# One-hop convolution shifts, scan pooling, paired output tiles and a GpSimd power for the norm scales, in an eight-core encoder step

## The chip, the cores and the metric

The kernel runs as one program on all eight cores of a Trainium2 chip; cores 0 to 3 are one die, 4 to 7 the other. Each core takes its own part of the tokens. The metric is the device time of the slowest core in microseconds (us). Engines are named as in the profile: PE (TensorE matmuls), PEld (weight loads of TensorE), DVE (VectorE), ACT (ScalarE), POOL (GpSimd), SP (SyncE). L405 means line 405 of the kernel in question, so the same statement can have another number in another kernel.

The runs here fell into two states. In a slow run the cores of one die, or of both, show a lower granted TensorE clock than in the others, and the run is longer. All verdicts here compare fast runs with fast runs of the same chip and the same rounds.

## The reference, cut to what matters

Four layers, each with another token mixer, on x of D = 1024 channels; inner width E = 2048:

```python
def rms_norm(x, g):
    y = xf * lax.rsqrt(jnp.mean(xf * xf, axis=-1, keepdims=True) + EPS)
    return y * g
...
for i in range(4):
    h = rms_norm(x, g_norm[i]) * (1.0 + scale) + shift
    # 0: gMLP   1: short conv   2: GLU -> depthwise conv of 31 taps -> LayerNorm -> silu
    # 3: trailing means over 2, 4, 8, 16 positions, one per channel group, minus the token
    x = x + gate * einsum(y * silu(z), w_out[i])
return rms_norm(x, g_final), ...
```

Every `rsqrt` is of one number per token.

## The kernel before

Activations are transposed: channels on the 128 partitions, tokens along the free dimension. A core works through its tokens in two groups, of 1074 columns (three matmuls of 358) and 1056 (three of 352); the groups take turns, layer by layer. PE writes to two PSUM slots of three banks each, so at most two output tiles are open. Weights come through a ring of eight 512 KB slots that POOL's queue loads.

The norm of the next layer is woven as "hooks" into the eight output tiles `d` of the *other* group's output projection, so that PE has work while the norm is made:

```python
hooks = {0: [sq(0..7)],                     # ACT: squares
         1: [stats(0..7), rstd],            # PE: column sums into bank 6; then the scale
         3: [bc, apply(0)],                 # PE: spread the scale over 128 partitions
         4..6: two applications each, 7: one}
...
def rstd():                                 # q96 is [96, W]: 3 thirds of the tokens, 32 equal rows each
    dve.tensor_scalar_add(q96, PSB[0:96, 6, 0:W], EPS)
    dve.reciprocal(q96, q96)
    act.activation(q96, q96, Sqrt)
def bc():                                   # matmul with sel = 1/32 over the 32 equal rows
    for q in range(3): matmul(PSB[:, slot, 0:W], lhsT=sel[32*q:32*q+32, :], rhs=q96[32*q:32*q+32, :])
    act.activation(rb, PSB[:, slot], Copy)
```

The column sums come as 32 identical rows per third of the tokens. The LayerNorm of layer 2 (`finalize`) has the same reciprocal and root. The output projection finishes tile after tile; only its first tile takes its 16 products one by one as they become ready:

```python
for d in range(8):
    sl = next_slot()
    if d == 0: for e in eorder: tile_mm(sl, w[e], ys[e])     # waits per e
    else:      tile_mm(sl, all 16)
    dve: x[d] += gate * PSUM                                  # the eviction
    for fn in hooks[d]: fn()
```

The convolution of 31 taps runs on PE with four shifted copies of the data. Their making went through DRAM:

```python
sp.dma(g_dram[c % 4], G)                                      # hop 1: write 280 KB
for sft in range(4):                                          # hop 2: read back, shifted
    sp.dma(R[32*sft:32*sft+32, :, 0:RW], AP(g_dram, offset + sft, [[GW, 32], [32*GW, 4], [1, RW]]))
```

Pooling adds shifted copies, doubling the window each time (one add for 2, four for 16):

```python
while step < win:
    dve.tensor_tensor(d_[lo:wd], cur[lo:wd], cur[lo-step:wd-step], add);  step *= 2
```

## Time and profile before

| | before |
|---|---|
| runs | 2359.1, 2494.44 (slow), 2360.89 us |
| span of the profiled cores | 2344.8 to 2353.8 us, core 1 slowest |
| PE / DVE / ACT / POOL busy | 94 / 47 / 27 / 8% |
| sum of PE gaps of 0.6 us and more, core 1 (added up from PE's timeline) | 128.6 us, 45 of them in the first 370 us |

First the page of the kernel before: busy us with the share of the span, PE's busy tenths in 40 slices, and the shares of the chain that ended last.

```profile
PE 2202.8 (94%) x16875; PEld 1360.6 (58%) x16875; DVE 1097.1 (47%) x1603; ACT 634.4 (27%) x726; POOL 193.1 (8%) x336
...
PE   4999999989999999999999999899988989998995
...
PE 80%; DVE 8%; DMA 7%; ACT 2%; issue 2%; SPq 0%; POOL 0%; DVEq 0%; ACTq 0%; POOLq 0%
```

PE is busy almost everywhere, and the chain is PE's for four fifths. A change that removes no matmul can only close PE's gaps. What PE waits for is listed by releaser: us in total, how often, the longest.

```profile
PE ps L452 <- DVE ysT L951: 12.9, 8, 2.6
PE ps L886 <- DMA tmp<-gscr: 12.7, 6, 4.0
PE ps L452 <- ACT tmp L914: 10.6, 4, 4.8
PE ps L452 <- ACT tmp L1036: 9.3, 8, 2.0
...
PE ps L452 <- DVE xb_sb L512: 5.6, 4, 1.4
PE ps L452 <- DVE xa_sb L512: 4.9, 5, 1.3
```

These are small sums: products of layer 2 that come too slowly for its output projection (L951), the read-back of the shifted copies (gscr), the eviction held up at layer 2's statistics (L914), the eviction held up by the pooling adds (L1036), and the ordinary waits of an output projection for an eviction (L512). The timeline shows the third of them. Columns: start, duration, engine, line, operation, and in brackets the idle time before it and what ended it.

```profile
1420.94 2.39 DVE L924 RECIPROCAL tmp<-tmp 96x358 f32<-96x358 f32 x1
...
1423.40 1.28 ACT L925 ACT_TABLE_LOAD   x1 [4.21 <-DVE tmp L924]
1424.69 0.50 ACT L925 ACTIVATE tmp<-tmp 96x358 f32<-96x358 f32 x1
1425.22 1.28 ACT L914 ACT_TABLE_LOAD   x1
...
1427.72 6.43 PE L452 MATMUL ps<-hT,ring 128*128 128x358 bf16 x24 [4.80 <-ACT tmp L914]
```

The scale of 96x358 values costs 2.39 us of reciprocal, 0.50 us of root, and two loads of ACT's function table of 1.28 us. ACT could not evict the tile that PE had finished, so PE stood 4.80 us. The windows view: us, PE busy and count, the same for PEld, DVE, ACT, POOL, then the granted clock, DMA's share and GB/s.

```profile
1427.72:1431.72 4.00, 4.00 (x14) 2.06 (x15) 1.28 (x1) 0.81 (x1) 0.00 (x0) 0.50 0.00 0
1435.72:1439.72 4.00, 4.00 (x28) 2.54 (x26) 3.24 (x3) 2.16 (x3) 0.00 (x0) 1.00 0.00 0
```

What the trace has on a power (POOL's only arithmetic in this kernel, in groups: operation and shapes, count, busy us, mean ns of one, idle before):

```profile
L681 POOL TENSOR_TENSOR stat<-stat 128x1 f32<-128x1 f32 x17 | 23.1, 1359 | 136.7 <-DVE stat L680 136.7
```

It is a power of one column. Pooling, in PE's timeline of the 16-wide channels:

```profile
1914.87 7.52 PE L452 MATMUL ps<-hT,ring 128*128 128x358 bf16 x48 [1.40 <-ACT tmp L1036]
```

48 matmuls take 7.52 us, and then PE waits, since four adds of about 1.29 us and the rest of DVE's work take longer than that (the next tile starts 8.92 us after this one). Last, the shift copies in the list of DMA issues: count, KB each, median us from issue to landing.

```profile
tmp<-gscr SPq DMA_DIRECT2D x64, 278.5 KB, 5.6
...
gscr<-tmp SPq DMA_DIRECT2D x32, 280.0 KB, 7.3
```

### The profile page before, as it was taken

How to read it: one execution, taken by the hardware profiler on the slowest of the kernel's cores; microseconds unless marked ns; L12 is line 12 of the kernel's file. 1: busy time of each engine (PE TensorE's matmuls, PEld its weight loads, DVE VectorE, ACT ScalarE, POOL GpSimd, SP SyncE). 2: the span in 40 equal slices, each digit the busy share in tenths (PEclk: the TensorE clock that was granted, in tenths of full speed). 3: DMA queues.
4: the chain of work that ended last, by engine and by line, in shares of the span. 5: the costliest groups of instructions: out<-in, count | busy, mean ns of one | idle time of the engine just before them, and what ended most of it. 6: DMA issues, size and time to landing. Idle time of an engine off the chain costs nothing.

```text
span 2353.8 us, 41088 instructions; the slowest of 8 cores (2344.8 to 2353.8 us)
## 1 busy us (share of the span) xinstructions
PE 2202.8 (94%) x16875; PEld 1360.6 (58%) x16875; DVE 1097.1 (47%) x1603; ACT 634.4 (27%) x726; POOL 193.1 (8%) x336
## 2 busy tenths in 40 slices
PE   4999999989999999999999999899988989998995
PEld 2645655446666666666666665566655656665663
DVE  3354230642555545555552216552328476456645
ACT  2354312633011120111202235312345122212221
POOL 1012101121001000010000000000000000000000
PEclk9999999999999999999999999999999999999998
DMA  9907738077346443464447773558765334433424
GB/s 205 207 7 110 124 64 133 1 132 120 55 71 108 72 82 54 75 110 77 82 84 176 174 163 52 88 117 179 170 129 90 63 63 72 66 63 61 72 50 145
DMA packets 75639, 233.36 MB, mean 99 GB/s; under 512 B 9728, under 2 KB 10368, under 8 KB 75296
## 3 DMA queue, kind: packets, MB, share of 16 engines
q0 software_dynamic: 44928, 163.60, 41.6%
q1 hardware_dynamic: 30528, 67.15, 11.4%
q8 instruction: 136, 2.23, 0.4%
q14 instruction: 47, 0.39, 0.1%
HBM read 375.57 MB, written 18.73 MB: 168 GB/s over the span
## 4 chain that ended last, share of the span: by engine, by line
PE 80%; DVE 8%; DMA 7%; ACT 2%; issue 2%; SPq 0%; POOL 0%; DVEq 0%; ACTq 0%; POOLq 0%
PE ps L452 69%; PE ps L654 5%; PE ps L886 4%; DVE tmp L1056 3%; DMA gscr<-tmp 2%; DMA ring<-w_in_a 2%; DMA tmp<-gscr 2%; DMA ring<-w_ada 1%; DVE tmp L1063 1%; PE ps L723 1%; ACT tmp L1036 1%; PE ps L719 1%; DVE xb_sb L512 1%; DMA xa_sb<-xa 0%; PE ps L398 0%
## 5 line engine op out<-in xcount | busy, mean ns | idle before, releaser
L452 PE MATMUL ps<-hT,ring 128*128 128x358 bf16 (+1 forms) x8448 | 1311.2, 316 | 38.5 <-ACT tmp L914 10.6
L452 PEld LDWEIGHTS ps<-hT,ring 128*128 128x128 bf16 x8448 | 826.6, 98 | 515.1 <-issue 59.8
L452 PE MATMUL ps<-ysT,ring 128*128 128x352 bf16 (+1 forms) x3072 | 476.2, 315 | 22.3 <-DVE ysT L951 12.9
L452 PEld LDWEIGHTS ps<-ysT,ring 128*128 128x128 bf16 x3072 | 298.6, 98 | 199.6 <-issue 32.5
L886 PE MATMUL ps<-tmp 128*32 128x358 bf16 (+1 forms) x3072 | 129.0, 324 | 12.8 <-DMA tmp<-gscr 12.7
L847 DVE TENSOR_TENSOR tmp<-tmp,ps 128x1074 bf16<-128x1074 f32 (+3 forms) x64 | 45.4, 709 | 186.8 <-PE ps L452 183.5
L654 PE MATMUL ps<-ring,hT 128*128 128x512 bf16 (+1 forms) x576 | 127.1, 379 | 3.9 <-DMA ring<-w_in_a 2.6
L886 PEld LDWEIGHTS ps<-tmp 128*32 128x32 bf16 x3072 | 84.3, 98 | 55.6 <-issue 22.6
L512 DVE SCALAR_TENSOR_TENSOR xb_sb<-ps,modT,xb_sb 128x704 f32<-128x704 f32 (+2 forms) x96 | 56.1, 584 | 127.0 <-PE ps L452 120.3
L789 DVE TENSOR_TENSOR tmp<-tmp,ps 128x1074 f32<-128x1074 f32 (+3 forms) x64 | 45.4, 710 | 140.3 <-PE ps L452 136.6
L1056 DVE TENSOR_TENSOR tmp<-tmp 128x1088 f32<-128x1088 f32 (+5 forms) x80 | 102.8, 1285 | 5.1 <-DVE tmp L1056 0.2
L1036 ACT ACTIVATE tmp<-ps 128x1074 f32<-128x1074 f32 (+3 forms) x64 | 39.4, 616 | 242.1 <-PE ps L452 164.2
L891 ACT ACTIVATE ysT<-ps,cst_sb 128x1074 bf16<-128x1074 f32 (+3 forms) x64 | 45.2, 706 | 206.8 <-PE ps L886 203.8
L779 ACT ACTIVATE tmp<-ps 128x1074 f32<-128x1074 f32 (+1 forms) x32 | 33.9, 1059 | 247.9 <-PE ps L452 173.9
L512 DVE SCALAR_TENSOR_TENSOR xa_sb<-ps,modT,xa_sb 128x1074 f32<-128x1074 f32 x32 | 42.7, 1335 | 123.0 <-PE ps L452 123.0
L654 PEld LDWEIGHTS ps<-ring,hT 128*128 128x128 bf16 (+1 forms) x576 | 55.5, 98 | 68.9 <-issue 4.9
L806 DVE SCALAR_TENSOR_TENSOR tmp<-tmp,cst_sb 128x1074 f32<-128x1074 f32 (+1 forms) x64 | 85.1, 1329 | 6.7
L810 ACT ACTIVATE ysT<-ps 128x1074 bf16<-128x1074 f32 (+1 forms) x32 | 33.9, 1059 | 184.2 <-PE ps L452 184.1
L452 PE MATMUL ps<-tmp,ring 128*128 128x358 bf16 (+1 forms) x384 | 63.2, 323 | 12.6 <-DVE ysT L1015 8.9
L741 DVE TENSOR_TENSOR ysT<-ysT,tmp 128x1074 bf16<-128x1074 bf16 (+1 forms) x32 | 22.8, 714 | 106.4 <-ACT tmp L740 106.4
L813 DVE TENSOR_TENSOR tmp<-tmp,ps 128x1074 f32<-128x1074 f32 (+3 forms) x64 | 45.4, 709 | 55.7 <-PE ps L452 52.0
L872 DVE TENSOR_TENSOR tmp<-dmask,cst_sb 128x1024 bf16<-128x1024 bf16 x32 | 39.2, 1225 | 59.1 <-PE ps L886 56.9
(151 smaller groups left out, 1562.9 us busy)
## 6 DMA issues: line engine op xcount, KB each, us to landing
ring<-w_in_b POOLq DMA_DIRECT2D x64, 512.0 KB, 5.4
ring<-w_ada POOLq DMA_DIRECT2D x48, 512.0 KB, 9.7
ring<-w_in_a POOLq DMA_DIRECT2D x48, 512.0 KB, 13.2
ring<-w_in_c POOLq DMA_DIRECT2D x48, 512.0 KB, 7.2
tmp<-gscr SPq DMA_DIRECT2D x64, 278.5 KB, 5.6
tmp<-gscr SPq DMA_DIRECT2D x64, 275.5 KB, 5.9
ring<-w_in_d POOLq DMA_DIRECT2D x32, 512.0 KB, 5.2
gscr<-tmp SPq DMA_DIRECT2D x32, 280.0 KB, 7.3
```

The lines of the kernel that those rows point to most:

```text
L452: ins = h.matmul(PSB[:, 3 * sl + n, 0:W], lhsT=lw, rhs=rh[:, n * W:(n + 1) * W], start=(first and k == 0), stop=(last and k == len(pairs) ...
L512: s.op("dve", lambda h, ps=ps, xv=xv, smp=smp, d=d: h.scalar_tensor_tensor(out=xv, in0=ps, scalar=gate[:, 16 + d, smp:smp + 1], in1=xv, op ...
L654: ins = h.matmul(PSB[0:n, nq, :], lhsT=hT[:, kh * 4 + kk, hc:hc + n], rhs=vw[nq * 2 + kh][:, kk, :], start=(kh == 0 and kk == 0), stop=(kh ...
L789: s.op("dve", lambda h, ps=ps, cc=cc, n=n, nb=nb, smp=smp, p=p, CG=CG: h.tensor_tensor(out=shp(p[:, H + cc + smp * H:H + cc + smp * H + n] ...
L806: s.op("dve", lambda h, p=p, a=a, c=c, wd=wd, k=k: h.scalar_tensor_tensor(out=a[:, 0:wd], in0=p[:, k:k + wd], scalar=prmT[:, c, k:k + 1], ...
L813: s.op("dve", lambda h, ps=ps, cc=cc, n=n, nb=nb, smp=smp, a=a, CG=CG: h.tensor_tensor(out=shp(tf(CG + cc, n), nb), in0=shp(a[:, cc + smp ...
L847: s.op("dve", lambda h, ps=ps, cc=cc, n=n, nb=nb, smp=smp: h.tensor_tensor(out=shp(G[:, H + cc + smp * H:H + cc + smp * H + n], nb), in0=s ...
L872: s.op("dve", lambda h: h.tensor_tensor(out=wd, in0=mk, in1=wrepT[:, c, :].unsqueeze(2).broadcast_to([128, 32, 32]), op=ALU.mult), reads=[ ...
L886: ins = h.matmul(PSB[32 * j:32 * j + 32, 3 * sl + n, 0:WC], lhsT=wd[:, b, j, :], rhs=R[:, j, 4 * b + n * WC:4 * b + (n + 1) * WC], start=( ...
L891: s.op("act", lambda h, ps=ps, cc=cc, n=n, nb=nb: h.activation(out=shp(ysT[:, c, cc:cc + n], nb), in_=ps, func=AF.Identity, bias=prmT[:, c ...
L1036: s.op("act", lambda h, ps=ps, cc=cc, n=n, nb=nb, smp=smp, pv=pv: h.activation(out=shp(pv[:, H + cc + smp * H:H + cc + smp * H + n], nb), ...
L1056: s.op("dve", lambda h, d_=d_, cur=cur, lo=lo, step=step: h.tensor_tensor(out=d_[:, lo:wd], in0=cur[:, lo:wd], in1=cur[:, lo - step:wd - s ...
```

## The change

The intent was to free PE of its gaps: shifts in one hop from SBUF to SBUF, pooling in one scan instead of up to four adds, two output tiles filled in turn so that PE has twice the work per product that arrives, and the scales as `x ** -0.5` on POOL, which has little to do, so that DVE loses a reciprocal and ACT a root with its table loads. The norm's hooks move back by one tile to fit the pairs. The diff, cut:

```diff
 def rstd():
     dve.tensor_scalar_add(q96, PSB[0:96, 6, 0:W], EPS)
-    s.op("dve", lambda h: h.reciprocal(out=q96, in_=q96), ...)
-    s.op("act", lambda h: h.activation(out=q96, in_=q96, func=AF.Sqrt), ...)
+    s.op("pool", lambda h: h.tensor_tensor(out=q96, in0=q96, in1=stat[0:96, 20:21].broadcast_to([96, W]), op=ALU.pow), ...)
 # ... the same in finalize() of layer 2; stat[:, 20] holds -0.5

 # output projection
+first = [next_slot(), next_slot()]
+for i, e in enumerate(eorder):
+    for d in range(2):
+        tile_mm(first[d], WT[g], [(ws[d][0][:, e, :], ysT[:, e, 0:NCOL[g]])], ..., i == 0, i == 15)
 for d in range(8):
-    ... one tile at a time, d == 0 by single e
+    ... d < 2: already done; else one tile at a time

 # norm hooks
-    1: stats + rstd,  3: bc, apply(0),  4..6: two applications each, 7: one
+    2: stats + rstd,  4: bc, apply(0),  5: apply 1, 2, 3,  6: 4, 5,  7: 6, 7

 # conv shifts
-s.dma("sp", ..., g_dram[c % 4], G, ...)
-for sft in range(4): s.dma("sp", ..., R[32*sft:32*sft+32, :, 0:RW], AP(g_dram, offset + sft, [[GW, 32], [32*GW, 4], [1, RW]]))
+for j in range(4):
+    g = G[32*j:32*j+32, 0:RW]
+    s.dma("sp", ..., R[:, j, 0:RW], AP(g.tensor, g.offset, [g.ap[0], [1, 4], [1, RW]]))
 # ... mask and tap layout permuted to match

 # pooling
-while step < win: dve.tensor_tensor(add); step *= 2
+if win == 2: dve.tensor_tensor(out=cur, in0=pv, in1=pad[PD-1:...], add)
+else:        dve.tensor_tensor_scan(out=cur, data0=pv, data1=pad[PD-win:...], op0=add, op1=subtract)
 # ... three input buffers instead of two; ACT copies the history
```

More of the change, by code (lines that the diff above doesn't have):

```diff
@@ L203, in build_program @@
         st_out[l] = (dout(nm + "_p", [128, 16 * HIST[l]]), dout(nm + "_s", [128, 16 * HIST[l]]))
-    g_dram = [nc.dram_tensor("gscr%d" % i, [128, GW], BF16, kind="Internal").ap() for i in range(4)]
     s = Sched(nc)
@@ L328, in build_program, with f_mask @@
     s.op("act", lambda h: h.activation(out=sc32[:, :, 0:2], in_=cT, func=AF.Silu), reads=["cst0", "sc32"], writes=["sc32"])
-    for q in range(4):
-        s.op("dve", lambda h, q=q: h.tensor_copy(out=dmask[32 * q:32 * q + 32, :], in_=ident[32 * q:32 * q + 32, 32 * q:32 * q + 32]),
-             reads=["ident"], writes=["dmask"])
+    def f_mask(h):
+        with nc.allow_low_precision(reason="a 0/1 mask"):
+            return h.tensor_reduce(out=dmask, in_=ident.rearrange("p (m s) -> p m s", s=4), axis=AX, op=ALU.add)
+    s.op("dve", f_mask, reads=["ident"], writes=["dmask"])
     def ada_mm(l, part, AT):
@@ L404, in rstd @@
             s.op("dve", lambda h: h.tensor_scalar_add(out=q96, in0=PSB[0:96, 6, 0:W], scalar1=EPS), writes=bk(6) + qk)
-            s.op("dve", lambda h: h.reciprocal(out=q96, in_=q96), reads=qk, writes=qk)
-            s.op("act", lambda h: h.activation(out=q96, in_=q96, func=AF.Sqrt), reads=qk, writes=qk)
+            s.op("pool", lambda h: h.tensor_tensor(out=q96, in0=q96, in1=stat[0:96, 20:21].broadcast_to([96, W]), op=ALU.pow), reads=qk + ["neghalf"], writes=qk)
         def bc():
@@ L496, in out_phase, with weights @@
         eorder = [e for e in range(16) if e not in late] + list(late)
-        for d in range(8):
-            spec = ("out%d" % l, d, g)
-            w, wkey = get(spec)
-            w = v3(w, 16)
-            sl = next_slot()
-            pr = [(w[:, e, :], ysT[:, e, 0:NCOL[g]]) for e in eorder]
-            if d == 0:
-                for i, e in enumerate(eorder):
-                    tile_mm(sl, WT[g], pr[i:i + 1], [wkey, "ys.%d" % e], i == 0, i == 15)
-            else:
-                tile_mm(sl, WT[g], pr, [wkey] + ["ys.%d" % e for e in range(16)])
-            release(spec)
+        specs = [("out%d" % l, d, g) for d in range(8)]
+        def weights(d):
+            w, wkey = get(specs[d])
+            return v3(w, 16), wkey
+        first = [next_slot(), next_slot()]
+        ws = [weights(0), weights(1)]
+        for i, e in enumerate(eorder):
+            for d in range(2):
+                tile_mm(first[d], WT[g], [(ws[d][0][:, e, :], ysT[:, e, 0:NCOL[g]])], [ws[d][1], "ys.%d" % e], i == 0, i == 15)
+        for d in range(2):
+            release(specs[d])
+        for d in range(8):
+            if d < 2:
+                sl = first[d]
+            else:
+                w, wkey = weights(d)
+                sl = next_slot()
+                tile_mm(sl, WT[g], [(w[:, e, :], ysT[:, e, 0:NCOL[g]]) for e in eorder], [wkey] + ["ys.%d" % e for e in range(16)])
+                release(specs[d])
             x = xt[g]
@@ L859, in front @@
                      reads=tk(SIG, NC), writes=sk(sa) + ["oS2"])
-            s.dma("sp", "gw%d" % (c % 4), g_dram[c % 4], G, reads=gk, writes=["gd.%d" % (c % 4)])
         def spread(c):
@@ L864, in spread @@
             R = v3(tb(RB[ci], 4480), 4)
-            src = g_dram[c % 4]
-            for sft in range(4):
-                s.dma("sp", "gr%d_%d" % (ci, sft), R[32 * sft:32 * sft + 32, :, 0:RW],
-                      bass.AP(src.tensor, src.offset + sft, [[GW, 32], [32 * GW, 4], [1, RW]]),
-                      reads=["gd.%d" % (c % 4)], writes=["R%d.%d" % (ci, sft)] + (tk(RB[ci], 2240) if sft == 0 else []))
+            G = tb(GB[ci], GW)
+            for j in range(4):
+                g = G[32 * j:32 * j + 32, 0:RW]
+                s.dma("sp", "gr%d_%d" % (ci, j), R[:, j, 0:RW],
+                      bass.AP(g.tensor, g.offset, [list(g.ap[0]), [1, 4], [1, RW]]),
+                      reads=tk(GB[ci], 560), writes=["R%d.%d" % (ci, j)] + (tk(RB[ci], 2240) if j == 0 else []))
             wd = tb(WD[ci], 1024).rearrange("p (a b) -> p a b", a=32)
@@ L923, in finalize @@
             s.op("dve", lambda h: h.tensor_scalar(out=v, in0=v, scalar1=0.0, scalar2=EPS, op0=ALU.max, op1=ALU.add), reads=vk, writes=vk)
-            s.op("dve", lambda h: h.reciprocal(out=v, in_=v), reads=vk, writes=vk)
-            s.op("act", lambda h: h.activation(out=v, in_=v, func=AF.Sqrt), reads=vk, writes=vk)
+            s.op("pool", lambda h: h.tensor_tensor(out=v, in0=v, in1=stat[0:96, 20:21].broadcast_to([96, W]), op=ALU.pow), reads=vk + ["neghalf"], writes=vk)
         def bcast(src_o, dst_o):
@@ L1000, in in_phase3 @@
         wd = H + WB
-        PV, P1, P2, DL = (0, 1152), 2304, 3456, (4608, 4608 + 2176)
+        PV, SM, DL = (0, 1152, 2304), 3456, (4608, 4608 + 2176)
+        PD = 16
         corder = [c for gq in (3, 2, 1, 0) for c in range(4 * gq, 4 * gq + 4)]
@@ L1018, in pool_group @@
             release(spec)
+        for b in range(3):
+            s.op("dve", lambda h, b=b: h.memset(tf(PV[b], PD + H), 0.0), writes=tk(PV[b], PD + H))
         for j, c in enumerate(corder):
@@ L1026, in in_phase3 @@
             sp_ = inproj(g, v3(tl[0][0], 8), tl[0][1], c % 2, fine=(j == 0))
-            po = PV[j % 2]
-            pv = tf(po, 1104)
-            pk = tk(po, 1104)
-            if g == 0:
-                s.op("dve", lambda h, pv=pv: h.memset(pv[:, 0:H], 0.0), writes=pk)
-            else:
-                s.op("dve", lambda h, pv=pv, c=c: h.tensor_copy(out=pv[:, 0:H], in_=outP[3][:, c, :]), reads=["oP3"], writes=pk)
-                s.op("dve", lambda h, pv=pv, c=c: h.tensor_copy(out=pv[:, H + NPA:2 * H + NPA], in_=stT[:, c, HS[3]:HS[3] + H]), reads=["cst1"], writes=pk)
+            po = PV[j % 3]
+            pad = tf(po, PD + wd)
+            pv = pad[:, PD:PD + wd]
+            pk = tk(po, PD + wd)
+            if g == 1:
+                s.op("act", lambda h, pv=pv, c=c: h.activation(out=pv[:, 0:H], in_=outP[3][:, c, :], func=AF.Copy), reads=["oP3"], writes=pk)
+                s.op("act", lambda h, pv=pv, c=c: h.activation(out=pv[:, H + NPA:2 * H + NPA], in_=stT[:, c, HS[3]:HS[3] + H], func=AF.Copy), reads=["cst1"], writes=pk)
             for ps, cc, n, nb, smp in pieces(g, sp_, W, 0):
@@ L1046, in in_phase3 @@
                 s.op("dve", lambda h, pv=pv, c=c: h.tensor_copy(out=outS[3][:, c, :], in_=pv[:, NC + H:NC + 2 * H]), reads=pk, writes=["oS3"])
-            cur, ck = pv, pk
-            step = 1
-            bufs = [P1, P2]
-            bi = 0
-            while step < win:
-                o = bufs[bi]
-                bi ^= 1
-                d_ = tf(o, 1104)
-                lo = 2 * step - 1
-                s.op("dve", lambda h, d_=d_, cur=cur, lo=lo, step=step: h.tensor_tensor(
-                    out=d_[:, lo:wd], in0=cur[:, lo:wd], in1=cur[:, lo - step:wd - step], op=ALU.add), reads=ck, writes=tk(o, 1104))
-                cur, ck = d_, tk(o, 1104)
-                step *= 2
+            cur, ck = tf(SM, wd), tk(SM, wd)
+            if win == 2:
+                s.op("dve", lambda h, cur=cur, pad=pad, pv=pv: h.tensor_tensor(out=cur, in0=pv, in1=pad[:, PD - 1:PD - 1 + wd], op=ALU.add), reads=pk, writes=ck)
+            else:
+                s.op("dve", lambda h, cur=cur, pad=pad, pv=pv, win=win: h.tensor_tensor_scan(
+                    out=cur, data0=pv, data1=pad[:, PD - win:PD - win + wd], initial=0.0, op0=ALU.add, op1=ALU.subtract), reads=pk, writes=ck)
             dl = v3(tb(DL[gq % 2], 4 * 1074), 4)[:, c % 4, :]
@@ L1123, in norm_hooks @@
         hooks = {0: [lambda d=d: sq(d) for d in range(8)],
-                 1: [lambda d=d: stats(d) for d in range(8)] + [rstd],
-                 3: [bc, lambda: apply(0)]}
-        for d in range(4, 8):
-            hooks[d] = [lambda d=d: apply(2 * d - 7)] + ([lambda d=d: apply(2 * d - 6)] if d < 7 else [])
+                 2: [lambda d=d: stats(d) for d in range(8)] + [rstd],
+                 4: [bc, lambda: apply(0)]}
+        for d, which in ((5, (1, 2, 3)), (6, (4, 5)), (7, (6, 7))):
+            hooks[d] = [lambda i=i: apply(i) for i in which]
         return hooks
@@ L1212 @@
     wcc = np.concatenate([f("w_conv_c"), np.zeros((1, E), np.float32)], 0)
-    wrep = wcc.reshape(8, 4, 16, 4, 32).transpose(1, 4, 2, 0, 3).reshape(128, 16 * 32)
+    wrep = wcc.reshape(8, 4, 16, 4, 32).transpose(4, 1, 2, 0, 3).reshape(128, 16 * 32)
     fixed = {"gn": chan(f("g_norm"), 8), "bada": chan(f("b_ada"), 24), "gf": chan(f("g_final")[None], 8), "prm": chan(prm9, 16), "wrep": wrep}
```

## The prediction

> **What bounds the kernel.** TensorE: the page gives PE 94% busy, VectorE 47%, ScalarE 27%, GpSimd 8%; the chain of waits is 80% PE. A 358-column matmul follows its neighbour every 0.156 us (48 in 7.47 us), and the change removes no matmul. It can only close PE gaps. In core 1's PE timeline, gaps from 0.6 us up sum to 129 us, 45 of them in the start, which the change hardly touches.
>
> **Gaps that should go (about 50 us).**
> - Conv shifts: PE waits for the read-back from DRAM at 1249, 1263, 1408, 1597 and 1743 us, 12 us in all. In the chain the write takes 6.5-9.2 us, the read-back 6.1-12.2 us. About 15 us of PE work covers one hop: gain 12.
> - Pooling: with four 1.29 us adds, VectorE takes 8.93 us per tile of the 16-wide group (period in the chain) against 7.47 us of PE. PE gaps there, held-up evictions (3.8 and 3.4 us) included: about 16 us.[...] Gain 16.
> - Layer 2 statistics: reciprocal 2.39 us, two table loads of 1.28 us and the root 0.50 us hold up ScalarE's eviction; PE stands 4.8 us, twice. The last tiles feed the output projection every 3.2 us: gaps 1.0+2.6+2.6 and 1.1+2.5+2.1 us. Without the root, and with a second tile to fill, both close: gain 22.
>
> **New gaps (about 24 us).**
> - Paired tiles finish 0.47 us apart, both PSUM slots full. The third tile waits for the first eviction (1.34 us, or 0.95+0.55+0.25 in the second group): estimate 1.1 or 1.75 us in each of 8 output phases, 11 us.
> - The norm hooks move back: two applications (1.27+0.56 or 1.25+0.95 us each) instead of one follow the last eviction. The next layer's first matmuls wait for them: about 2 us more at 6 boundaries, 13 us with the last norm.
>
> **The power.** The trace shows it only on 128x1: 0.55 us[...].[...] Eight of its twelve uses have two output tiles (15 us) of cover; the start covers about 8 us, layer 2 about 6; the last norm is bare[...].
>
> **Time.** 2361 - 50 + 24 + 4 = 2339 us; 2318 to 2368 should hold it 8 times in 10. Faster by over 2%: 0.10; within 2%: 0.84; slower: 0.06.
>
> **What would show it.** Waits for shifted tiles gone. Pooling period 7.5 us[...]. No 4.8 us gap at the layer 2 statistics, no 2.6 us gaps before its output projection. A wait of 1-2 us for the eviction on every output phase's third tile; 1-2 us longer waits at layer boundaries.[...] ScalarE's root and its table loads gone.
>
> **What would make it wrong.** A power far over 15 us would stall every norm.[...] Shift copies from 32 partitions slower than about 11 us would keep the conv waits.

The sum came to 2339 us: 2361, less 50 for gaps that go, plus 24 for new gaps, plus 4 for the powers, all at the last norm. Terms are cut from the text above. What it said of the scan's length, and what it expected of the power on 96 partitions, with the loss of 4 us and the gain of some 10 that followed from it, rested on figures that no trace or run of this case shows. So the 4 can't be followed, and the gain of 16 stands for the sum of the pooling's PE gaps in the trace, if the scan is short enough to close them. On the one-column power the trace has more than one number: of 18, the three that began before DVE's L684 or within 0.04 us of its start took 0.55 to 0.56 us, and the 15 that began some 0.16 us into it took 1.53 to 1.55.

## The result, and the profile after

| | before | after |
|---|---|---|
| median of these runs | 2359.99 us | 2904.74 us |
| fast runs | 2359.1, 2360.89, 2356.84 | 2892.64, 2916.85, 2889.78 |
| slow runs | 2494.44 | 3112.42 |
| ratio of fast runs | | **1.2293** (95%: 1.219 to 1.2395) |
| spans of the profiled run | 2344.8 to 2353.8 us | 2877.3 to 2891.1 us |
| granted clock of the cores | 0.976 to 0.978 | 0.889 to 0.901 |

A ratio here is the mean time of one kernel's fast runs over that of the other's fast runs of the same rounds, so it is not quite the ratio of the medians quoted. The change made the kernel 23% slower; the prediction was 2339 us, and its range ended at 2368.

The page after, the same parts:

```profile
PE 2211.9 (77%) x16875; PEld 1359.4 (47%) x16875; DVE 1029.0 (36%) x1498; ACT 612.3 (21%) x729; POOL 879.0 (30%) x348
...
PE   1699949986699957999399929499846699399830
...
POOL 6302261124300062010800082600255300800257
PEclk7899969998799988999699969699968799699965
...
PE 67%; POOL 22%; DVE 4%; POOLq 2%; DMA 2%; ACT 1%; issue 1%; DVEq 0%; SPq 0%; ACTq 0%
```

PE does the same 16875 matmuls in nearly the same busy time, 2211.9 us against 2202.8, but holes have come into its row, and POOL's row has its high digits there. (The clock's row dips at the same places.) POOL, which was 0% of the chain, is 22% of it. POOL's groups by shape:

```profile
L405 POOL TENSOR_TENSOR tmp<-tmp,stat 96x352 f32<-96x352 f32 x5 | 282.2, 56444 | 35.8 <-DVE tmp L404 35.8
L405 POOL TENSOR_TENSOR tmp<-tmp,stat 96x358 f32<-96x358 f32 x4 | 229.8, 57460 | 31.2 <-DVE tmp L404 31.2
L405 POOL TENSOR_TENSOR tmp<-tmp,stat 96x384 f32<-96x384 f32 x1 | 61.5, 61543 | 8.4 <-DVE tmp L404 8.4
```

One power takes **56.4 to 61.5 us**, where I had estimated so much less that all twelve together were to cost 4 us. With the two of layer 2 the twelve take 687.3 us. PE's waits:

```profile
PE ps L413 <- POOL tmp L405: 461.3, 10, 58.0
PE ps L940 <- POOL tmp L932: 102.0, 2, 51.4
```

461.3 + 102.0 = 563.3 us of waits on powers, against a span that is 2891.1 - 2353.8 = 537.3 us longer. So the powers can explain all of the loss, and the rest of the change seems to have won some 26 us. (This is rough: the slow clock behind each wait, and the 13.5 us that PE waited behind the roots in before, are left out. The experiments below settle it.) The 687.3 us of powers less 563.3 us of waits leaves 124 us that PE's own work covered, 10 us each. One such hook in the timeline:

```profile
351.28 14.91 PE L451 MATMUL ps<-ysT,ring 128*128 128x358 bf16 x96
...
352.21 56.47 POOL L405 TENSOR_TENSOR tmp<-tmp,stat 96x352 f32<-96x352 f32 x1 [1.09 <-DVE tmp L404]
408.93 1.55 PE L413 MATMUL ps<-tmp,sel 32*128 32x352 f32 x6 [42.74 <-POOL tmp L405]
```

The two tiles of cover are there, 14.91 us, just as predicted. They cover a quarter of the power. Behind the wait the windows view again has half the clock (columns as before):

```profile
408.90:412.90 4.00, 3.97 (x15) 1.84 (x16) 1.05 (x1) 1.05 (x1) 0.87 (x2) 0.50 0.77 124
416.90:420.90 4.00, 4.00 (x28) 2.54 (x27) 1.37 (x2) 0.00 (x0) 0.53 (x1) 1.00 0.00 0
```

The other parts did what they were meant to. In PE's waits there is no line for a shifted tile any more, and the copies take one hop:

```profile
tmp<-tmp SPq DMA_DIRECT2D x64, 278.5 KB, 5.5
```

The scan took 2.42 us, where each of up to four adds took about 1.29 us in before:

```profile
L1060 DVE TENSOR_TENSOR_SCAN tmp<-tmp 128x1089 f32<-128x1089 f32 x12 | 29.1, 2421 | 0.0
```

And the third output tile of a projection waits for the first tile's eviction, estimated at 1.1 us, here 1.13:

```profile
1030.52 7.53 PE L451 MATMUL ps<-ysT,ring 128*128 128x358 bf16 x48 [1.13 <-DVE xa_sb L520]
```

### The profile page after: what moved, and what is told of

It is laid out like the page before. It is cut to its first block, busy times and chain, and to the rows that moved or that the text cites. A ratio compares the mean times of both kernels' runs of the same rounds, so it can differ in the third digit from the quotient of the medians.

```text
span 2891.1 us, 41033 instructions; the slowest of 8 cores (2877.3 to 2891.1 us)
## 1 busy us (share of the span) xinstructions
PE 2211.9 (77%) x16875; PEld 1359.4 (47%) x16875; DVE 1029.0 (36%) x1498; ACT 612.3 (21%) x729; POOL 879.0 (30%) x348
## 4 chain that ended last, share of the span: by engine, by line
PE 67%; POOL 22%; DVE 4%; POOLq 2%; DMA 2%; ACT 1%; issue 1%; DVEq 0%; SPq 0%; ACTq 0%
PE ps L451 56%; POOL tmp L405 18%; PE ps L894 4%; PE ps L662 4%; POOL tmp L932 4%; POOLq L1177 2%; DMA ring<-w_in_a 1%; DVE hT L420 1%; DVE xb_sb L520 1%; DMA xa_sb<-xa 1%; PE ps L731 1%; PE ps L727 1%; ACT hT L391 1%; DVE xa_sb L520 1%; PE ps L413 1%
## 5 line engine op out<-in xcount | busy, mean ns | idle before, releaser
L451 PE MATMUL ps<-hT,ring 128*128 128x358 bf16 (+1 forms) x8448 | 1311.4, 316 | 32.0 <-DVE hT L427 10.5
L405 POOL TENSOR_TENSOR tmp<-tmp,stat 96x352 f32<-96x352 f32 (+2 forms) x10 | 573.6, 57360 | 75.3 <-DVE tmp L404 75.3
L451 PE MATMUL ps<-ysT,ring 128*128 128x352 bf16 (+1 forms) x3072 | 487.3, 320 | 20.1 <-DVE xb_sb L520 7.1
L413 PE MATMUL ps<-tmp,sel 32*128 32x352 f32 (+2 forms) x60 | 15.7, 873 | 461.3 <-POOL tmp L405 461.3
L417 ACT ACTIVATE tmp<-ps 128x1056 f32<-128x1056 f32 (+2 forms) x10 | 10.7, 1066 | 726.5 <-PE ps L413 726.5
L123 POOL DMA_DIRECT2D ring<-w_in_c x48 | 25.5, 533 | 437.1 <-PE ps L451 420.5
L123 POOL DMA_DIRECT2D ring<-w_in_b x64 | 33.9, 532 | 368.7 <-PE ps L451 345.0
L932 POOL TENSOR_TENSOR tmp<-tmp,stat 96x358 f32<-96x358 f32 (+1 forms) x2 | 113.9, 56946 | 19.6 <-DVE tmp L931 19.6
L420 DVE TENSOR_TENSOR hT<-xa_sb,tmp 128x1074 bf16<-128x1074 f32 (+1 forms) x32 | 40.7, 1291 | 196.6 <-ACT tmp L417 196.6
L420 DVE TENSOR_TENSOR hT<-xb_sb,tmp 128x1056 bf16<-128x1056 f32 x32 | 40.0, 1251 | 176.8 <-ACT tmp L417 176.8
L797 DVE TENSOR_TENSOR tmp<-tmp,ps 128x1074 f32<-128x1074 f32 (+3 forms) x64 | 45.4, 709 | 141.2 <-PE ps L451 137.5
## 6 DMA issues: line engine op xcount, KB each, us to landing
tmp<-tmp SPq DMA_DIRECT2D x64, 278.5 KB, 5.5
```

The lines of the kernel that those rows point to most:

```text
L123: h.dma_start(out=out, in_=in_, **kw).then_inc(dsm, 16)
L405: s.op("pool", lambda h: h.tensor_tensor(out=q96, in0=q96, in1=stat[0:96, 20:21].broadcast_to([96, W]), op=ALU.pow), reads=qk + ["neghalf" ...
L413: ins = h.matmul(PSB[:, 3 * sl + q, 0:W], lhsT=sel[32 * q:32 * q + 32, :], rhs=tf(QD, W)[32 * q:32 * q + 32, :], start=True, stop=True)
L420: s.op("dve", lambda h: h.tensor_tensor(out=hT[:, d, c0:c0 + n], in0=x[:, d, c0:c0 + n], in1=rb, op=ALU.mult), reads=["x%d.%d" % (g, d)] + ...
L451: ins = h.matmul(PSB[:, 3 * sl + n, 0:W], lhsT=lw, rhs=rh[:, n * W:(n + 1) * W], start=(first and k == 0), stop=(last and k == len(pairs) ...
L797: s.op("dve", lambda h, ps=ps, cc=cc, n=n, nb=nb, smp=smp, p=p, CG=CG: h.tensor_tensor(out=shp(p[:, H + cc + smp * H:H + cc + smp * H + n] ...
```

## The experiments

The profile after names its suspect clearly. Still, a wait that a trace puts down to one engine is not yet a cause, and three questions needed the chip. (1) Is the power's own length the whole of the loss, or do the moved hooks and the paired tiles make it dear, by leaving it less cover? (2) What is the power's price made of: a fixed cost per instruction, the values that the kernel needs, or the columns of each partition, copies included? (3) What are the other three parts worth, and does the slower clock behind a wait explain where they differ from my sums?

The first four kernels ran on a chip that was not settled: the kernel before itself ran there from 2381 to 2689 us with one die or the other at a lower clock, and no ratio was formed. For these four I quote die 0 in runs in which it was undisturbed; the kernel before has 2341 to 2358 us there. Three of the four were repeated on another chip.

### The power taken out: no_power, and again as no_power_again

```diff
 # the kernel after, both places
-pool.tensor_tensor(q96, q96, -0.5, op=pow)
+dve.reciprocal(q96, q96)
+act.activation(q96, q96, Sqrt)
```

> The change with VectorE's reciprocal and ScalarE's root put back at both places, everything else of the change kept. Theory A (the power's length is the whole loss, the rest is a gain): the twelve PE waits on the power, 563 us in the profile after, and PE's half clock behind each of them, some 2 us, go; the waits of 4.8 us at the layer 2 statistics and the 3 us at the last norm come back. About 2325 us, 2308 to 2345. Rival B (something else of the change costs too: the pairs, the moved hooks, the shift copies): 2361 us or more.

Measured: median 2368.71 us on the unsettled chip; die 0 took 2321 to 2335 us, that is some 20 us less than before.

> The same kernel as no-power: its first chip was unsettled (the kernel before at 2396 us median there, and no ratio of fast runs could be formed). Theory A, from its undisturbed die (2324 to 2331 us) and from the three parts measured alone (ratios 0.9923, 0.9890, 1.0084, product 0.990): ratio 0.986 to 0.993, about 2330 us. Rival B: above 1.00.

Measured: fast runs 2335.36, 2336.6 and 2361.8 us, ratio 0.9945 (0.987 to 1.002). The third fast run had two cores of one die at a clock of 0.970 to 0.972 instead of 0.983, so it is the two others that show the undisturbed kernel: about 1% under the 2355.74 to 2362 us of most of the fast runs of before. With the third run the ratio lies just outside the 0.986 to 0.993 that I had expected. In its waits, those of layer 2's statistics are back:

```profile
PE ps L452 <- ACT tmp L923: 12.4, 6, 4.8
```

What follows: without the power, everything else in the change makes the kernel a little faster or leaves it equal. The whole loss of more than 530 us is the power's. The theory that pairs or hooks cost it is out.

### The power alone: power_alone

```diff
 # the kernel before, both places
-dve.reciprocal(q96, q96)
-act.activation(q96, q96, Sqrt)
+pool.tensor_tensor(q96, q96, -0.5, op=pow)
```

> The kernel before with only the power on GpSimd put in, at both places. Theory A: eight norms with two output tiles of cover stall PE by about 43 us, the start by about 50, the two layer 2 statistics by about 47 each, the last norm by about 55, and PE restarts slowly each time: 2361 + 550 = about 2910 us, 2880 to 2940, power instructions of 56 to 62 us. Rival B (the power is slow because of what the rest of the change puts beside it, or the rest makes its stalls longer): clearly under 2850 us.

Measured: median 2944.33 us, fast runs 2935.37 and 2939.57 us; die 1 was disturbed (clock 0.880 to 0.890 against 0.889 to 0.899), and die 0 took about 2896 to 2908 us, some 550 us more than before's die 0. Its waits:

```profile
PE ps L413 <- POOL tmp L405: 460.2, 10, 57.5
PE ps L931 <- POOL tmp L923: 101.9, 2, 51.4
```

562.1 us, with the old hooks and without pairs, against 563.3 us with the new ones. So the place of the hooks does not matter for this loss: in both there are two tiles between the power and its use. The number of 2944 itself is a little over my 2910, and I put nothing on that difference, because of the chip.

### Half of the columns: half_power, and again as half_again

The power takes half of the columns; DVE and ACT do the other half as before, at the same time.

```diff
-pool.tensor_tensor(q96, q96, -0.5, pow)
+pool.tensor_tensor(q96[:, 0:W//2], ..., pow)
+dve.reciprocal(q96[:, W//2:W], ...);  act.activation(q96[:, W//2:W], ..., Sqrt)
+act: a one-value copy that waits for both halves
```

> The changed kernel with the power on the first half of the columns only; VectorE's reciprocal and ScalarE's root do the other half at the same time. Theory A (0.30 us and 0.159 us for each column, from the three widths in the profile after): 28.4 to 30.9 us for each instruction, every one of the twelve waits 28 us shorter, 2905 - 12 x 28.5 = about 2560 us, 2535 to 2590. Rival C (a fixed cost of an instruction, or time in which another engine holds GpSimd up): instructions of about 57 us still, 2880 us or more.

Measured on the unsettled chip: 2599 to 2888 us; die 0, where undisturbed, 2553 to 2565 us.

> The same kernel as half-power, for the same reason; its undisturbed die took 2556 to 2565 us there. Theory A: 2550 to 2575 us. Rival C: 2880 us or more.

Measured: fast runs 2567.75 and 2566.05 us, ratio 1.0867 (1.081 to 1.0924). POOL's group:

```profile
L406 POOL TENSOR_TENSOR tmp<-tmp,stat 96x179 f32<-96x179 f32 x4 | 115.6, 28906 | 31.6 <-DVE tmp L404 31.6
```

Half of the columns cost half: 28.9 us instead of 57.5. From the widths of the kernel after, (61.543 - 56.444) / (384 - 352) = 0.159 us per column, and 56.444 - 352 x 0.1593 = 0.4 us is left for the start of the instruction. A large fixed cost per instruction is out.

### Fewer columns, the same values: spread_power, and again as spread_again

Half the columns is also half of the values that the kernel needs, so half_again can't tell those two apart. Of the 96 rows only three are distinct, and what is needed is about 1074 values. In this kernel a DMA lays one copy of the values out over 96 partitions in 11 or 12 columns, POOL takes the power of that, and a second DMA lays them back into three rows. All values that the kernel needs are still made; the copies are not.

```diff
-pool.tensor_tensor(q96, q96, -0.5, pow)                      # [96, W]
+sp.dma(pq, rows.rearrange("q (r k) -> q r k", r=32))         # 3 rows -> [96, 12]
+pool.tensor_tensor(pq, pq, -0.5, pow)
+sp.dma(rows.rearrange("q (r k) -> q r k", r=32), pq)
 # bc: one row per matmul instead of 32 equal ones, times 32 in the copy
```

> The changed kernel with the power kept on GpSimd, but one copy of the 1074 values laid out by a small transfer as 96 partitions of 12 columns, and brought back by another. Theory A (the cost goes with the columns of a partition, not with the values that are needed): power instructions of about 2.2 us (0.3 + 12 x 0.159)[...], all twelve long waits of PE gone: about 2325 us, 2305 to 2345. Rival C (a fixed cost of an instruction): 57 us still, 2880 us or more.

Measured on the unsettled chip: median 2389.23 us; die 0 2336 to 2349 us.

> The same kernel as spread-power, for the same reason. Theory A: the twelve long waits gone,[...] a power of 2.3 us where the root was; the start waits 14 us for it and the last norm 8: 5 to 15 us slower than the no-power kernel, ratio 0.990 to 0.998.

Measured: fast runs 2348.88, 2349.02, 2352.91 and 2351.16 us, ratio 0.9951 (0.9916 to 0.9986). POOL's groups and PE's waits for the way back:

```profile
L413 POOL TENSOR_TENSOR tmp<-tmp,stat 96x12 f32<-96x12 f32 x5 | 11.5, 2298 | 65.6 <-DMA tmp<-tmp 65.6
L413 POOL TENSOR_TENSOR tmp<-tmp,stat 96x11 f32<-96x11 f32 x5 | 10.7, 2134 | 60.8 <-DMA tmp<-tmp 60.8
```

```profile
PE ps L422 <- DMA tmp<-tmp: 22.3, 2, 13.8
...
PE ps L958 <- DMA tmp<-tmp: 7.5, 2, 4.3
```

The 12-column power took 2.30 us and the 11-column one 2.13: again 0.16 us per column. The price goes by the columns of a partition, copies included, and not by the values that are needed: 358 columns were paid for where 12 hold them all. (All these powers span 96 partitions, so columns and the values that POOL works through rise together, and these runs can't tell those two apart. The one-column power on 128 partitions took 0.55 us at its shortest, which is what 0.4 + 0.159 us for one column gives.) Eight of the twelve waits are gone. What remains is the start (13.8 us), the last norm (8.4 us), which have little or no cover, and layer 2 (7.5 us). As a repair it is no better than the reciprocal and the root: 2348.9 to 2352.9 us here, 2335.4 and 2336.6 there, with the two hops of DMA in place of two short instructions.

### The clock behind a wait: warm_wait

In the kernel after, eight of the hooks' waits are filled with matmuls on a spare bank whose result nobody reads. The outputs stay right. If the slow restart came of the matmuls behind the wait themselves (their weights, their inputs), it would stay; if it comes of PE having stood idle, it would go.

```diff
+def fill(k): k times matmul(PSB[:, 7, 0:256], lhsT=flat[:, 0:128], rhs=flat)
-    4: [bc, apply(0)]
+    4: [fill(385 if g == 1 else 402), bc, apply(0)]
```

> The changed kernel with idle matmuls on the free eighth bank that fill nearly all of the eight waits for the power in the output phases (385 or 402 of 0.109 us each, 42 or 44 us). Theory D (a long wait costs more than its length, because the granted clock is half for 2 to 5 us behind it): behind those eight waits the clock reads 1.00 instead of 0.50, and the time falls by 8 x 2 = about 16 us, to about 2885 us. Rival E (the waits cost their length alone): no change, 2900 us. Rival F (the half clock follows the power on GpSimd, not PE's idleness): 0.50 behind the waits still.

Measured: fast runs 2873.14 and 2874.42 us, ratio 1.2166 (1.2102 to 1.223); three of five runs were slow, 3274 to 3342 us at a clock near 0.80 on one die. The windows view of the stretch behind the same wait (columns as before), and the timeline:

```profile
409.50:413.50 4.00, 3.96 (x27) 2.38 (x28) 1.61 (x2) 1.05 (x1) 0.88 (x2) 1.00 0.65 118
```

```profile
409.54 0.87 PE L413 MATMUL ps<-tmp,sel 32*128 32x352 f32 x6 [0.71 <-POOL tmp L405]
```

The power is still as long, and the broadcast still waits for it. But its six matmuls took 0.87 us instead of 1.55, and PE did 27 matmuls in the next 4 us instead of 15, at a clock of 1.00 instead of 0.50. (The 385 matmuls of the filling cut PE's wait from the 42.74 us of after to 0.71 us, so they took about 0.109 us each.) The best fast run came out 16.6 us under the best of after (2873.14 against 2889.78; other chips, so only the size counts): about 2 us for each of eight waits. The other waits bear it out. In the 4 us behind the wait the clock is 1.00 at all eight filled waits of this trace and 0.50 at its four unfilled ones (start, layer 2 twice, last norm); in after's trace it is 0.50 to 0.58 at all twelve. So here it is idleness that costs the clock, not the matmuls that follow, and not the power on POOL, which runs at all twelve. In after's trace the clock behind this wait is 0.50 for the first 4 us, 0.93 for the next 4, then 1.00. The filling is not a repair: the power's wait stays, and three of these five runs were slow (of after, one of four; too few to say whether the filling does that).

### Each other part alone: one_hop, scan, pairs

These three went to a third chip together, where the kernel before had a median of 2355.69 us. Each is the kernel before with one part of the change.

```diff
 # one_hop: before, with the four SBUF-to-SBUF copies in place of gscr, mask and taps permuted
```

> The kernel before with only the one-hop conv shifts. Theory A: the five PE waits on the read-back, 12 us in the profile before, go: about 2349 us, 2344 to 2354. Rival: copies out of 32 partitions that take over 11 us would keep the waits: 2361 us.

Measured: median 2339.12 us, ratio 0.9923 (0.9905 to 0.994), so 18 us won, where I had summed 12. No wait of PE for a shifted tile is left.

```diff
 # scan: before, with tensor_tensor_scan, three buffers, ACT copying the history
```

> The kernel before with only the scan pooling. Theory A: the pooling layer's PE gaps, about 16 us, go; period per tile of the 16-wide group 7.5 us instead of 8.9: about 2345 us, 2340 to 2350. Rival: VectorE was not what held PE there: 2361 us.

Measured: fast runs 2329.16 and 2331.78 us (four of six were slow), ratio 0.989 (0.9864 to 0.9916), so 26 us won, where I had summed 16. (The kernel also moves DVE's copies of the history to ACT; no run separates that from the scan.) PE no longer pauses between the tiles of the 16-wide channels:

```profile
1882.99 41.10 PE L452 MATMUL ps<-hT,ring 128*128 128x358 bf16 x267 [0.85 <-DVE tmp L1022]
```

```diff
 # pairs: before, with the two first tiles filled in turn and the hooks moved back
```

> The kernel before with only the paired output tiles and the moved norm hooks. Theory A: gains about 11 us in front of layer 2's output projection, loses 11 us at eight third tiles and 13 us at six layer boundaries and the last norm: about 2374 us, 2364 to 2380. Rival (VectorE catches up, the pairs are a gain as the change intends): under 2358 us.

Measured: median 2378.1 us, fast runs 2372.53 to 2380.37, ratio 1.0084 (1.006 to 1.0108), so 20 us **lost**, where I had summed a loss of 12 (24 less the 12 of the gaps in front of layer 2's output projection). Its waits show both sides:

```profile
PE ps L452 <- DVE xb_sb L521: 12.7, 8, 1.8
...
PE ps L452 <- DVE hT L428: 10.5, 9, 1.6
...
PE ps L452 <- DVE xa_sb L521: 8.8, 9, 1.1
```

The line L951 of before (12.9 us) is gone, as hoped. But the waits for evictions have grown from 5.6 + 4.9 to 12.7 + 8.8 us, 11.0 more, which is what I had predicted for the third tiles; and the next layer's first matmul waits 10.5 us for the late applications (L428), where before has 1.8. Besides, waits for the evictions of the next layer's first tiles, which DVE now reaches later, add up to some 7 us more.

Where do the three differ from my sums? The same comparison for every profiled run: span of the slowest core, PE's gaps of 0.6 us and more summed from its timeline, and PE's busy time. All do the same matmuls, except for what is missing in a trace (17 records in that of scan, 2.7 us at 0.156 us each).

| kernel | span | PE gaps | PE busy |
|---|---|---|---|
| before | 2353.8 | 128.6 | 2202.8 |
| one_hop | 2337.4 | 122.2 | 2195.4 |
| scan | 2327.6 | 113.7 | 2190.5 |
| pairs | 2372.5 | 149.4 | 2201.4 |
| no_power_again | 2333.8 | 123.7 | 2189.9 |
| rearranged (below) | 2291.2 | 88.7 | 2181.8 |
| after | 2891.1 | 660.7 | 2211.9 |

The loss of pairs, 18.7 us of span, is all in its gaps (+20.8). The gain of scan is not: its gaps fell by 14.9 us, close to my 16, and the busy time of the same matmuls fell by another 12.3 us, or some 9.6 with the missing records allowed for. With one_hop the gaps fell by 6.4 (the copies' 12.3 us in such gaps are gone, but in this trace waits in the first 600 us, which differ from run to run, were 4.3 us longer, and those of the pooling 1.6 us) and the busy time by 7.4. In before's trace most gaps of 1.9 us and more are followed by a clock of 0.50 for 3 to 5 us, so that closing such a gap gave back more than its length. That is where, in before, the convolution's tile of 96 matmuls took 5.5 to 5.6 us behind three of its five waits; in one_hop's second group it takes 3.90 us, one after the other. Not every gap does this. In the same trace, gaps of 1.8 us and less that stood alone were followed by the full clock, all but one (1.14 us, at 484 us). Most of those of 1.9 to 4.8 us were followed by the half one, but gaps of 2.41, 2.04 and 2.56 us were not, nor two of 2.04 and 3.75 us between the short bursts of the first 30 us.

### Put together otherwise: rearranged

Can the good parts be had without the bad ones? This kernel keeps the one-hop copies and the scan, and puts the reciprocal and root back. It makes the pair less even, so that the two first tiles end apart and the third needn't wait; starts the applications one tile earlier; and in layer 2 it issues the root after the eviction that it used to hold up.

```diff
 # the kernel after
-pool power, both places
+dve.reciprocal; act Sqrt (in layer 2 the Sqrt comes after the eviction of zmm(3))
-for i, e in enumerate(eorder): for d in range(2): ...
+steps = tile 0 with the first 12 e, tile 1 with the first 12, tile 0 with the last 4, tile 1 with the last 4
-    4: [bc, apply(0)],  5: apply 1, 2, 3,  6: 4, 5,  7: 6, 7
+    3: [bc, apply(0)],  4..6: two applications each,  7: one
```

> One hop, scan and pairs, no power: reciprocal and root as before, the root placed behind the next eviction on ScalarE, the first output tile of a pair finished before the last four inputs of the second, and the norm hooks so that one application follows the last eviction, as before. Theory A: the no-power kernel less about 8 us at third tiles, 11 us at the boundaries and 6 us at the layer 2 statistics: about 2305 us, 2290 to 2318. Rival: those waits are not on PE's path: the same as the no-power kernel.

Measured: 2292.78, 2294.88, 2291.5 and 2292.26 us, all fast; before's median on that chip was 2355.69 us; ratio **0.973** (0.9713 to 0.9748). It beats both kernels. Its waits:

```profile
PE ps L452 <- DVE xb_sb L522: 7.3, 8, 1.4
...
PE ps L452 <- DVE xa_sb L522: 4.9, 5, 1.3
PE ps L452 <- ACT tmp L924: 4.5, 4, 1.8
```

The evictions' waits are nearly those of before (7.3 and 4.9 us, against 12.7 and 8.8 with even pairs), and the 4.8 us stops at the statistics are no longer in the list. In the timeline the third tile's wait, 1.13 us in the first group and 1.76 in the second with even pairs, is gone in the first group and 0.4 us in the second. Of the 63 us, one_hop and scan alone account for 18 and 26; the other 19 or so belong to the uneven pair, the hooks and the later root together, and no run tells those three apart. The table above splits it the other way: gaps -39.9 us, busy time of the same matmuls -21.0 us.

## Why the prediction was wrong, point by point

**The bound and the rule of the game were right.** PE bounds the kernel; the change could only close or open PE's gaps, and PE's busy time rose by only 9 us.

**The failed step: the estimate of the power's length.** A power measured 56.4 to 61.5 us, where the estimate let all twelve together cost 4 us. I had a power of one column in the trace (0.55 us at its shortest), which can't tell a start-up from a price per column. Then I took a time of another operation, which no run here shows, and multiplied it by a guess. A power costs 159 ns per column here. Nothing in the trace spoke for my factor. The range that I gave said that I knew the order of magnitude, and I didn't.

**The mechanism was right, and so was the cover.** I wrote that eight uses have 15 us of cover, the start 8, layer 2 about 6 and the last norm none, and that "a power far over 15 us would stall every norm". That is what happened: 14.91 us of cover in the hook shown, and 51.0 us of wait for 57 us of power in layer 2. With the measured powers in the prediction's own sum: 8 x (57 - 15) + (61.5 - 8) + 2 x (57 - 6) + 56.4 = 548 us on top of 2361 - 50 + 24 = 2335 gives 2883 us; the fast runs took 2890 to 2917. Only this one term was mis-sized by more than some 10 us. Power_alone and no_power_again show that it is that term, and spread_again that its size comes from the columns, most of them copies.

**Conv shifts: right, undersized.** Waits gone; 18 us won, not 12. **Pooling: right, undersized.** The scan took 2.42 us, 1.9 times the 1.285 us of an add of that width, in place of up to four of those. 26 us won, not 16. The missing term in both is the half clock behind a gap: the timeline of before had it in plain sight, 24 matmuls in 6.43 us instead of 3.85, and I counted only the gap.

**Layer 2 statistics: half right.** The pairs closed the gaps before the output projection (12.9 us). The 4.8 us stops were not closed but became 51 us each. The root and its table loads did go: 26 table loads in before's trace, 9 in after's.

**Pairs and hooks: right in kind, undersized.** The third tile's waits cost 11.0 us more than before, as predicted. The moved hooks cost more than the 13 us: 8.7 us for the applications, some 7 us for the first tiles' evictions behind them, and a few more in places that I had not named. The net was a loss of 20 us and not of 12.

**The rest of the sum.** Leaving the power out and the 4.8 us stops in, the prediction's sum would be 2361 - 50 + 10 + 24 = 2345 us, and no_power_again's undisturbed runs took 2335 and 2337. That looks better than it is: two gains were too small and one loss was too small.

## What to carry to other kernels

Before work moves to another engine, look for a duration of that operation *on that engine at that shape*; if the trace has only a one-element case, measure it first, or give a range that admits not knowing it, and ask of a broadcast operand how many of its elements are copies. In a kernel bound by TensorE, look for the slow clock behind each gap and count both: here the changes that closed gaps of about 2 us and more won more than the sum of the gaps (in rearranged 39.9 us of gaps, and 21.0 us of busy time besides). And filling two tiles in turn also ends them together: in rearranged they end apart, and the third tile hardly waits.

## Durations and clocks measured here

- A `pow` of float32 on POOL over 96 partitions took 0.159 us per column and about 0.4 us besides: 2.13 us for 11 columns and 2.30 for 12 (spread_again), 28.9 for 179 (half_again), 57.5 for 358 and 61.5 for 384 (after). For 358 columns DVE's reciprocal and ACT's root took 2.39 + 0.50 us, with up to two table loads of 1.28 us (before).
- In the trace of before most gaps of PE of 1.9 us and more were followed by a clock of 0.50 for 3 to 5 us, and some of the same length (2.04, 2.41, 2.56 us) by 1.00; why equal gaps end differently was not shown. PE's busy time times the missing share of the clock, added up over windows of 1 us, comes to some 36 of before's 2353.8 us, 1.5%, as an estimate. The 21.0 us by which PE's busy time fell are a third of what rearranged won.
- A copy from SBUF to SBUF with a pattern of four shifts took 5.5 us at the median for 278.5 KB (after), about the same as reading it back from DRAM (5.6 us, before).
